# A batched x·yᵀ kernel on one core: TensorE's unrolled stream becomes a loop of three iterations over four groups of 8 heads, with credit semaphores

## The chip, the cores and the metric

The kernel runs on one core of a Trainium2 chip. The metric is the device time of one execution in microseconds, the median of several. A run is compared with executions of the kernel before in the same rounds on the same chip.

Short names: PE is TensorE's matrix multiply and PEld its weight load, DVE is VectorE, ACT is ScalarE, POOL is GpSimd, and SP is SyncE, which issues the DMAs.

## The reference

```python
x, y: (8, 12, 512, 64) float32          # batch, heads, rows, channels
out = np.einsum('bhtc,bhsc->bhts', x, y)  # (8, 12, 512, 512) float32
```

There are 96 independent products of 512x64 by 64x512. The inputs are 25 MB and the output is 101 MB, so the output dominates the traffic.

## The kernel before

Twelve groups of eight heads are handled one after the other. For each group the kernel loads x and y as 128 partitions of 4 KB rows (`a` selects one of two tiles of four heads), casts them to bf16 on GpSimd, transposes them on TensorE and copies them out of PSUM as `xT` and `yT`. Then it runs 16 matmul steps. A step is 8 matmuls into a PSUM tile of 128x1024, which ACT and DVE copy in turn into an output tile of 4 MB. The output tile is stored by one DMA; the first and the last tile are stored in four pieces of 1 MB. Tile, the framework, orders all of this and sets the semaphores.

```python
for g in range(NG):                                   # 12 groups
    steps = prepare(g + 1, made) ...                  # loads, casts, transposes of the next group
    for a in range(2):
        ot = opool.tile([P, R, S], fp32)              # 4 MB, three buffers
        for k in range(K):                            # 8 steps
            if k in (0, 3, 6): next(steps, None)
            pm = pmpool.tile([P, 2, S], fp32)         # three buffers
            for two in range(2):
                for h in range(G):                    # 4 heads: 32 columns of weights each
                    nc.tensor.matmul(pm[h*Q:(h+1)*Q, two, :],
                                     xT[a*C:(a+1)*C, 2*k+two, h*Q:(h+1)*Q],
                                     yT[a*C:(a+1)*C, h*S:(h+1)*S], start=True, stop=True)
            # ACT (even k) or DVE (odd k) copies pm into ot
        nc.sync.dma_start(ov[g, a], otf)              # (...) four pieces at both ends
```

## Time and profile before

| | before |
|---|---|
| time, median | 307.29 us of 3 runs (307.26 to 307.49) |
| span of the profiled execution | 305.6 us |
| instructions | 4,378, of which 3,840 are TensorE's matmuls and weight loads |
| DMA | 126.11 MB, 413 GB/s on average |

These lines of the page of the kernel before give, in order, the span, busy time of each engine, the DMA engines' busy tenths and their GB/s in 40 equal slices, and two DMA queues (packets, MB, share of 16 engines' span).

```profile
span 305.6 us, 4378 instructions
PE 203.8 (67%) x1920; PEld 91.5 (30%) x1920; DVE 138.4 (45%) x120; ACT 119.6 (39%) x121; POOL 49.3 (16%) x54
...
DMA  7999999999999999999999999999999999999980
GB/s 278 412 409 420 459 419 399 470 418 388 446 455 388 440 446 398 441 429 437 427 424 442 420 427 430 411 454 420 437 435 425 427 442 422 437 437 422 409 368 39
...
q1 hardware_dynamic: 10848, 125.83, 97.2%
q8 instruction: 15, 0.25, 0.3%
```

No compute engine is busy for more than two thirds of the span. DMA is at 90% or more in all but the first slice and the last two. (Bytes are counted in the slice in which their packet starts, so a single slice can read high: 16 engines that move 32 KB in 1213 ns each make 432 GB/s.) Queue q8 carries instruction fetches, 15 blocks of 16 KB. The waits view of the same kernel agrees (engine, line, what it waited for; us in total, times, longest).

```profile
ACT ot L129 <- DMA out_dram<-ot: 72.1, 11, 9.9
...
PE pm L122 <- ACT ot L129: 64.7, 14, 9.7
DVE ot L131 <- DMA out_dram<-ot: 63.4, 15, 9.3
```

ACT and DVE wait for a store to land before they may refill an output buffer, and PE waits behind ACT.

The following windows of the kernel before give the stretch, its length, busy time of each engine, the granted clock, the DMA share and GB/s.

```profile
290.00:295.00 5.00, 0.00 (x0) 0.00 (x0) 0.00 (x0) 0.00 (x0) 0.00 (x0) 0.50 1.00 423
...
297.00:298.00 1.00, 0.00 (x0) 0.00 (x0) 0.00 (x0) 0.00 (x0) 0.00 (x0) 0.50 0.50 213
...
300.00:301.00 1.00, 0.00 (x0) 0.00 (x0) 0.00 (x0) 0.00 (x0) 0.00 (x0) 0.50 0.06 25
...
303.00:304.00 1.00, 0.00 (x0) 0.00 (x0) 0.00 (x0) 0.00 (x0) 0.00 (x0) 0.50 0.06 25
304.00:305.00 1.00, 0.00 (x0) 0.00 (x0) 0.00 (x0) 0.00 (x0) 0.00 (x0) 0.50 0.00 0
```

A share of 0.06 is one DMA engine of 16. From 300 to 304 us the whole kernel waits for a single DMA engine. By the packet records it had no more to move than the others: its packets of 32 KB are 176 of 2,816, a sixteenth. So this one was slower. We call it the **late engine**.

**How the late engine was followed.** The trace has a record of every DMA packet (start, duration, size, queue), without the engine's number. On a busy engine a packet starts 3 to 4 ns before the one ahead of it ends, and the sizes of the packets are on record (a store of 4 MB is 128 packets of 32 KB, of which the chain has eight). So the chain can be followed back from the very last packet. In the kernel before it is a chain without a gap (but for one 0.3 us interruption by a packet of queue q14) from 1.88 us to 304.22 us. A 32 KB packet takes 1213 ns on nearly all engines. On the late engine it takes that too at times, but mostly 50 to 90 ns more. These durations are our own sums over the packet records, as no view prints them.

### The profile page before, as it was taken

The page shows a single profiled execution, that of the slowest core. Times are in us where ns is not written, and L with a number is a line of the kernel's source. Part 1 is how long each engine was busy: PE and PEld are TensorE (multiplying, and loading weights), DVE is VectorE, ACT ScalarE, POOL GpSimd, SP SyncE. Part 2 cuts the span into 40 slices and gives each one's busy share as a digit, 9 for nine tenths or more (in the row PEclk, how much of TensorE's full clock was granted, in tenths as well). Part 3 has the DMA queues.
Part 4 walks back from the last instruction along what each step waited for, and adds up shares of the span by engine and source line. Part 5 has one row for each costly group of instructions (what it writes and reads, how often), then busy time and mean ns, then how long its engine had stood idle before and what let it go on. Part 6 is the DMA issues. An engine that isn't in the chain of part 4 may idle for free.

```text
span 305.6 us, 4378 instructions
## 1 busy us (share of the span) xinstructions
PE 203.8 (67%) x1920; PEld 91.5 (30%) x1920; DVE 138.4 (45%) x120; ACT 119.6 (39%) x121; POOL 49.3 (16%) x54
## 2 busy tenths in 40 slices
PE   1899999969919928936932990991785976575000
PEld 1443234525404503512511540350251432222000
DVE  0465654657416507615633741670664664446000
ACT  1445527544523606505522451560653463325000
POOL 3755024300500500320140050041000000000000
PEclk9999999975555555755675555575575555555555
DMA  7999999999999999999999999999999999999980
GB/s 278 412 409 420 459 419 399 470 418 388 446 455 388 440 446 398 441 429 437 427 424 442 420 427 430 411 454 420 437 435 425 427 442 422 437 437 422 409 368 39
DMA packets 10867, 126.11 MB, mean 413 GB/s; under 512 B 864, under 2 KB 864, under 8 KB 7008
## 3 DMA queue, kind: packets, MB, share of 16 engines
q1 hardware_dynamic: 10848, 125.83, 97.2%
q8 instruction: 15, 0.25, 0.3%
q14 instruction: 4, 0.03, 0.0%
HBM read 25.17 MB, written 100.66 MB: 412 GB/s over the span
## 4 chain that ended last, share of the span: by engine, by line
DMA 49%; PE 29%; DVE 5%; issue 4%; ACT 3%; POOL 1%; SPq 0%; ACTq 0%
DMA out_dram<-ot 47%; PE pm L122 23%; DVE ot L131 5%; PE pt L95 4%; ACT ot L129 3%; PE pt L82 2%; DMA xs<-in_x_dram 2%; ACT xT L102 1%; POOL xb L73 1%; DVE xT L100 0%; SPq L55 0%; ACTq L129 0%; SPq L136 0%
## 5 line engine op out<-in xcount | busy, mean ns | idle before, releaser
L122 PE MATMUL pm<-yT,xT 64*32 64x512 bf16 x1536 | 159.4, 586 | 67.2 <-ACT ot L129 64.7
L131 DVE COPY ot<-pm 128x1024 f32<-128x1024 f32 x96 | 117.0, 1224 | 123.0 <-DMA out_dram<-ot 63.4
L129 ACT ACTIVATE ot<-pm 128x1024 f32<-128x1024 f32 x96 | 95.9, 1023 | 115.5 <-DMA out_dram<-ot 72.1
L122 PEld LDWEIGHTS <-xT 64*32 64x32 bf16 x1536 | 53.3, 118 | 148.1 <-issue 136.3
L73 POOL CAST yb<-ys 128x1024 bf16<-128x1024 f32 x24 | 24.3, 1040 | 143.5 <-PE pt L82 69.8
L82 PE MATMUL pt<-ident,yb 128*128 128x128 bf16 x192 | 23.9, 297 | 8.5 <-POOL yb L73 6.8
L102 ACT ACTIVATE xT<-pt 128x1024 bf16<-128x1024 bf16 x12 | 12.3, 1023 | 37.0 <-PE pt L95 30.3
L95 PE MATMUL pt<-ident,xb 128*128 128x128 bf16 x192 | 25.8, 310 | 1.3 <-DVE xT L100 0.8
L73 POOL CAST xb<-xs 128x1024 bf16<-128x1024 f32 x24 | 24.3, 1040 | 13.7 <-issue 4.9
L95 PEld LDWEIGHTS <-xb 128*128 128x128 bf16 x192 | 19.4, 143 | 22.7 <-issue 20.0
L82 PEld LDWEIGHTS <-yb 128*128 128x128 bf16 x192 | 19.3, 138 | 17.7 <-issue 8.2
L88 DVE COPY yT<-pt 128x1024 bf16<-128x1024 bf16 x12 | 14.6, 1216 | 8.5 <-PE pt L82 8.5
L90 ACT ACTIVATE yT<-pt 128x1024 bf16<-128x1024 bf16 x12 | 12.2, 1019 | 8.2 <-PE pt L82 8.2
L100 DVE COPY xT<-pt 128x1024 bf16<-128x1024 bf16 x12 | 8.3, 690 | 12.3 <-PE pt L95 9.8
L90 ACT ACT_TABLE_LOAD x1 | 1.3, 1283 | 0.7 <-PEq L151 0.7
masks.py:199 POOL TENSOR_SCALAR_AFFINE_SELECT ident<-ident 128x128 bf16<-128x128 bf16 x1 | 0.3, 292 | 0.1
masks.py:197 POOL MEMSET ident<- 128x128 bf16 x1 | 0.2, 204 | 0.3 <-POOLq L151 0.3
L151 POOL MEMSET const-float32-0.0<- 128x1 f32 x1 | 0.1, 98 | 0.2 <-issue 0.2
L151 POOL MEMSET const-bfloat16-1.0<- 128x1 bf16 x1 | 0.1, 101 | 0.0
L151 POOL MEMSET const-uint8-127<- 128x1 uint8 x1 | 0.1, 101 | 0.0
L151 POOL MEMSET const-float32-1.0<- 128x1 f32 x1 | 0.1, 98 | 0.0
## 6 DMA issues: line engine op xcount, KB each, us to landing
out_dram<-ot SPq DMA_DIRECT2D x22, 4096.0 KB, 27.4
ys<-in_y_dram SPq DMA_DIRECT2D x12, 1024.0 KB, 21.2
xs<-in_x_dram SPq DMA_DIRECT2D x12, 1024.0 KB, 23.4
out_dram<-ot SPq DMA_DIRECT2D x8, 1024.0 KB, 19.2
```

The costliest lines, as they stand in the source:

```text
L73: nc.gpsimd.tensor_copy(b[:, rows], s[:, :, rows].rearrange("p a r c -> p r a c"))
L82: nc.tensor.transpose(pt[:, k, :], yb[:, half * K + k].rearrange("p a c -> p (a c)"), ident)
L88: nc.vector.tensor_copy(dst, src)
L90: nc.scalar.activation(dst, src, COPY)
L95: nc.tensor.transpose(pt[:, k, :], xb[:, half * K + k].rearrange("p a c -> p (a c)"), ident)
L100: nc.vector.tensor_copy(dst, pt)
L102: nc.scalar.activation(dst, pt, COPY)
L122: nc.tensor.matmul(pm[h * Q:(h + 1) * Q, two, :], xT[a * C:(a + 1) * C, 2 * k + two, h * Q:(h + 1) * Q], yT[a * C:(a + 1) * C, h * S:(h + ...
L129: nc.scalar.activation(ot[:, 2 * k:2 * k + 2, :], pm, COPY)
L131: nc.vector.tensor_copy(ot[:, 2 * k:2 * k + 2, :], pm)
L151: nc = _bacc.Bacc("TRN2", target_bir_lowering=False, num_devices=1)
```

## The change

The intent is to save instruction fetches: TensorE gets a loop of three iterations whose body is four groups, and the other engines stay unrolled. The waits in this loop body are written with fixed counts, the same in all three iterations, so TensorE takes *credits*: it waits for a semaphore to be at least 1 (or 4) and subtracts that again. Tile cannot express this, so everything sits in one critical section with hand-made semaphores.

```diff
-    for g in range(NG):
-        (...)                       # Tile's pools, tiles and waits
+    with tc.tile_critical():
+        (...)                       # 32 semaphores, SP and POOL unrolled
+        def take(name, n=1):
+            pe.wait_ge(S_(name), n)
+            pe.sem_inc(S_(name), -n)
+        (...)
+        with pe.Fori(0, NG // BODY):              # 3 iterations
+            for i in range(BODY):                 # 4 groups
+                t = i % NT
+                take("T", 4)                      # all four copies of this group
+                for n in range(2 * K):
+                    a, k = divmod(n, K)
+                    if n in AT:                   # n = 2, 5, 8, 11
+                        transposes(i + 1, AT[n])  # takes c.. and pt..; a 13th, empty group at the end
+                    m = (i * 2 * K + n) % 3
+                    take(f"pm{m}")
+                    (...)                         # the same 8 matmuls
+                    ins.then_inc(S_("ma" if k % 2 == 0 else "mv"), 1)
+        (...)                       # ACT and DVE unrolled:
+            copy(eng, dst, src).then_inc(S_(f"pt{j % 2}"), 1)
+            eng.drain().then_inc(S_("T"), 1)
```

Data, layouts, buffers and DMA sizes stay. The load of a later group is issued somewhat later than before (SP's timeline has the fourth load of y at 12.01 us, not 7.75): behind the store of the group's first tile, and after the transposes that free its buffer.

More of the change, by code (lines that the diff above doesn't have):

```diff
@@ L6 @@
 from concourse._compat import with_exitstack
-from concourse.masks import make_identity
 @with_exitstack
@@ L31 @@
     K = R // 2
-    AHEAD = 3
+    BODY = 4
+    NL = 3
+    NO = 3
+    NT = 2
     fp32 = mybir.dt.float32
@@ L35 @@
     COPY = mybir.ActivationFunctionType.Copy
-    assert C * 2 == P and S == T and R == 16
+    assert C * 2 == P and S == T and R == 16 and NG % BODY == 0
     xv = x.rearrange("b h t c -> (b h t c)").rearrange("(g a p n) -> g p a n", a=2, p=P, n=R * C)
     yv = y.rearrange("b h t c -> (b h t c)").rearrange("(g a p n) -> g p a n", a=2, p=P, n=R * C)
-    ov = out.rearrange("b h t s -> (b h t s)").rearrange("(g a p n) -> g a p n", a=2, p=P, n=R * S)
-    const = ctx.enter_context(tc.tile_pool(name="const", bufs=1))
@@ L43 @@
-    lpool = ctx.enter_context(tc.tile_pool(name="lpool", bufs=AHEAD))
-    bpool = ctx.enter_context(tc.tile_pool(name="bpool", bufs=2))
-    tpool = ctx.enter_context(tc.tile_pool(name="tpool", bufs=2))
-    opool = ctx.enter_context(tc.tile_pool(name="opool", bufs=3))
-    ptpool = ctx.enter_context(tc.tile_pool(name="ptpsum", bufs=2, space=bass.MemoryType.PSUM))
-    pmpool = ctx.enter_context(tc.tile_pool(name="pmpsum", bufs=3, space=bass.MemoryType.PSUM))
-    loaded = {}
-    def load(g):
-        xs = lpool.tile([P, 2, R, C], fp32)
-        ys = lpool.tile([P, 2, R, C], fp32)
-        nc.sync.dma_start(ys.rearrange("p a r c -> p a (r c)"), yv[g])
-        nc.sync.dma_start(xs.rearrange("p a r c -> p a (r c)"), xv[g])
-        loaded[g] = (xs, ys)
@@ L59 @@
-    for g in range(AHEAD):
-        load(g)
-    ident = const.tile([P, P], bf16)
-    make_identity(nc, ident)
-    def prepare(g, made):
-        xs, ys = loaded.pop(g)
-        yb = bpool.tile([P, R, 2, C], bf16)
-        xb = bpool.tile([P, R, 2, C], bf16)
-        for s, b in ((ys, yb), (xs, xb)):
-            for half in range(2):
-                rows = slice(half * K, (half + 1) * K)
-                nc.gpsimd.tensor_copy(b[:, rows], s[:, :, rows].rearrange("p a r c -> p r a c"))
-        if g + AHEAD < NG:
-            load(g + AHEAD)
-        yield
-        yT = tpool.tile([P, G * Q, R], bf16)
-        xT = tpool.tile([P, R, P], bf16)
-        for half in range(2):
-            pt = ptpool.tile([P, K, P], bf16)
+    ov = out.rearrange("b h t s -> (b h t s)").rearrange("(o p n) -> o p n", p=P, n=R * S)
@@ new lines @@
+    sb = ctx.enter_context(tc.tile_pool(name="sb", bufs=1))
+    ps = ctx.enter_context(tc.tile_pool(name="ps", bufs=1, space=bass.MemoryType.PSUM))
+    ident = sb.tile([P, P], bf16)
+    xs = sb.tile([P, NL, 2, R, C], fp32)
+    ys = sb.tile([P, NL, 2, R, C], fp32)
+    xb = sb.tile([P, NT, R, 2, C], bf16)
+    yb = sb.tile([P, NT, R, 2, C], bf16)
+    xT = sb.tile([P, NT, R, P], bf16)
+    yT = sb.tile([P, NT, G * Q, R], bf16)
+    ot = sb.tile([P, NO, R, S], fp32)
+    pt = ps.tile([P, 2, K, P], bf16)
@@ new lines, with S_, store_cuts, load @@
+    pm = ps.tile([P, 3, 2, S], fp32)
+    sem = {}
+    def S_(name):
+        if name not in sem:
+            sem[name] = tc.alloc_semaphore(name)
+        return sem[name]
+    def store_cuts(o):
+        n = 4 if o in (0, 2 * NG - 1) else 1
+        return [(i * R // n, (i + 1) * R // n) for i in range(n)]
+    landed = [16 * sum(len(store_cuts(i)) for i in range(o % NO, o + 1, NO)) for o in range(2 * NG)]
+    with tc.tile_critical():
+        for name in ("ident", "T", "ma", "mv", "oa", "ov"):
+            S_(name)
+        for j in range(4):
+            S_(f"t{j}")
+            for t in range(NT):
+                S_(f"c{j}{t}")
+        for i in range(NL):
+            S_(f"ldx{i}"), S_(f"ldy{i}")
+        for i in range(NO):
+            S_(f"st{i}")
+        for i in range(2):
+            S_(f"pt{i}")
+        for i in range(3):
+            S_(f"pm{i}")
+        def load(g):
+            i = g % NL
+            if g >= NL:
+                nc.sync.wait_ge(S_("t1"), g - NL + 1)
+                nc.sync.wait_ge(S_("t3"), g - NL + 1)
+            nc.sync.dma_start(ys[:, i].rearrange("p a r c -> p a (r c)"), yv[g]).then_inc(S_(f"ldy{i}"), 16)
+            nc.sync.dma_start(xs[:, i].rearrange("p a r c -> p a (r c)"), xv[g]).then_inc(S_(f"ldx{i}"), 16)
+        for g in range(NL + 1):
+            load(g)
+        done = 0
+        for o in range(2 * NG):
+            if o % 2 == 1 and o // 2 + NL + 1 < NG:
+                load(o // 2 + NL + 1)
+            of = ot[:, o % NO].rearrange("p r s -> p (r s)")
+            for a, b in store_cuts(o):
+                done += 1
+                nc.sync.wait_ge(S_("oa"), done)
+                nc.sync.wait_ge(S_("ov"), done)
+                nc.sync.dma_start(ov[o][:, a * S:b * S], of[:, a * S:b * S]).then_inc(S_(f"st{o % NO}"), 16)
+        for o in range(2 * NG - NO, 2 * NG):
+            nc.sync.wait_ge(S_(f"st{o % NO}"), landed[o])
+        nc.gpsimd.memset(ident, 0.0).then_inc(S_("ident"), 1)
+        nc.gpsimd.wait_ge(S_("ident"), 1)
+        nc.gpsimd.affine_select(
+            out=ident, in_=ident, compare_op=mybir.AluOpType.not_equal, fill=1.0, base=0,
+            pattern=[[-1, P]], channel_multiplier=1,
+        ).then_inc(S_("ident"), 1)
+        for g in range(NG + 1):
+            i, t = g % NL, g % NT
+            for j in range(4):
+                s, b, ld = ((ys, yb, "ldy"), (xs, xb, "ldx"))[j // 2]
+                if j % 2 == 0 and g < NG:
+                    nc.gpsimd.wait_ge(S_(f"{ld}{i}"), 16 * (g // NL + 1))
+                if g >= NT:
+                    nc.gpsimd.wait_ge(S_(f"t{j}"), g - NT + 1)
+                if g < NG:
+                    rows = slice(j % 2 * K, (j % 2 + 1) * K)
+                    nc.gpsimd.tensor_copy(
+                        b[:, t, rows], s[:, i, :, rows].rearrange("p a r c -> p r a c")
+                    ).then_inc(S_(f"c{j}{t}"), 1)
+                else:
+                    nc.gpsimd.sem_inc(S_(f"c{j}{t}"), 1)
+        pe = nc.tensor
+        def take(name, n=1):
+            pe.wait_ge(S_(name), n)
+            pe.sem_inc(S_(name), -n)
+        def transposes(i, j):
+            t, b = i % NT, (yb, xb)[j // 2]
+            take(f"c{j}{t}")
+            take(f"pt{j % 2}")
@@ L81, in prepare @@
             for k in range(K):
-                nc.tensor.transpose(
-                    pt[:, k, :], yb[:, half * K + k].rearrange("p a c -> p (a c)"), ident
-                )
-            dst = yT[:, :, half * K:(half + 1) * K]
-            src = pt.rearrange("p k n -> p n k")
-            if half == 0:
-                nc.vector.tensor_copy(dst, src)
-            else:
-                nc.scalar.activation(dst, src, COPY)
-            yield
-        for half in range(2):
-            pt = ptpool.tile([P, K, P], bf16)
-            for k in range(K):
-                nc.tensor.transpose(
-                    pt[:, k, :], xb[:, half * K + k].rearrange("p a c -> p (a c)"), ident
-                )
-            dst = xT[:, half * K:(half + 1) * K]
-            if half == 0:
-                nc.vector.tensor_copy(dst, pt)
-            else:
-                nc.scalar.activation(dst, pt, COPY)
-            yield
@@ L104, in prepare @@
-        made[g] = (xT, yT.rearrange("p n k -> p (n k)"))
-    made = {}
-    for _ in prepare(0, made):
-        pass
-    for g in range(NG):
-        xT, yT = made.pop(g)
-        steps = prepare(g + 1, made) if g + 1 < NG else iter(())
-        for a in range(2):
-            ot = opool.tile([P, R, S], fp32)
-            otf = ot.rearrange("p r s -> p (r s)")
-            edge = (g == 0 and a == 0) or (g == NG - 1 and a == 1)
-            for k in range(K):
-                if k in (0, 3, 6):
-                    next(steps, None)
-                pm = pmpool.tile([P, 2, S], fp32)
-                for two in range(2):
-                    for h in range(G):
-                        nc.tensor.matmul(
-                            pm[h * Q:(h + 1) * Q, two, :],
-                            xT[a * C:(a + 1) * C, 2 * k + two, h * Q:(h + 1) * Q],
-                            yT[a * C:(a + 1) * C, h * S:(h + 1) * S],
-                            start=True, stop=True,
-                        )
-                if k % 2 == 0:
-                    nc.scalar.activation(ot[:, 2 * k:2 * k + 2, :], pm, COPY)
-                else:
-                    nc.vector.tensor_copy(ot[:, 2 * k:2 * k + 2, :], pm)
-                if edge and k % 2 == 1:
-                    i, j = (2 * k - 2) * S, (2 * k + 2) * S
-                    nc.sync.dma_start(ov[g, a][:, i:j], otf[:, i:j])
-            if not edge:
-                nc.sync.dma_start(ov[g, a], otf)
@@ new lines, in transposes @@
+                ins = pe.transpose(
+                    pt[:, j % 2, k], b[:, t, j % 2 * K + k].rearrange("p a c -> p (a c)"), ident
+                )
+            ins.then_inc(S_(f"t{j}"), 1)
+        pe.wait_ge(S_("ident"), 2)
+        for i in range(2):
+            pe.sem_inc(S_(f"pt{i}"), 1)
+        for i in range(3):
+            pe.sem_inc(S_(f"pm{i}"), 1)
+        for j in range(4):
+            transposes(0, j)
+        AT = {2: 0, 5: 1, 8: 2, 11: 3}
+        with pe.Fori(0, NG // BODY):
[8 more added lines that the diff above has]
+                    take(f"pm{m}")
+                    for two in range(2):
+                        for h in range(G):
+                            ins = pe.matmul(
+                                pm[h * Q:(h + 1) * Q, m, two, :],
+                                xT[a * C:(a + 1) * C, t, 2 * k + two, h * Q:(h + 1) * Q],
+                                yT[a * C:(a + 1) * C, t, h * Q:(h + 1) * Q].rearrange("c n k -> c (n k)"),
+                                start=True, stop=True,
+                            )
+                    ins.then_inc(S_("ma" if k % 2 == 0 else "mv"), 1)
@@ new lines, in copy, with evacuate @@
+        def copy(eng, dst, src):
+            if eng is nc.scalar:
+                return eng.activation(dst, src, COPY)
+            return eng.tensor_copy(dst, src)
+        def evacuate(eng, g, j):
+            t = g % NT
+            eng.wait_ge(S_(f"t{j}"), g + 1)
+            if g == NG:
+                if j < 2:
+                    eng.sem_inc(S_(f"pt{j}"), 1)
+                return
+            if j < 2:
+                dst, src = yT[:, t, :, j * K:(j + 1) * K], pt[:, j].rearrange("p k n -> p n k")
+            else:
+                dst, src = xT[:, t, (j - 2) * K:(j - 1) * K], pt[:, j - 2]
+            copy(eng, dst, src).then_inc(S_(f"pt{j % 2}"), 1)
+            eng.drain().then_inc(S_("T"), 1)
@@ new lines @@
+        for eng, first, ready, stored in (
+            (nc.vector, 1, "mv", "ov"),
+            (nc.scalar, 0, "ma", "oa"),
+        ):
+            mine = (0, 2) if eng is nc.vector else (1, 3)
+            for j in mine:
+                evacuate(eng, 0, j)
+            waiting = []
+            for o in range(2 * NG):
+                g, a = divmod(o, 2)
+                if o >= NO:
+                    eng.wait_ge(S_(f"st{o % NO}"), landed[o - NO])
+                cuts = [b for _, b in store_cuts(o)]
+                for k in range(first, K, 2):
+                    n = a * K + k
+                    m = (g % BODY * 2 * K + n) % 3
+                    for at, j in AT.items():
+                        if j in mine and at in (n, n - 1):
+                            evacuate(eng, g + 1, j)
+                    eng.wait_ge(S_(ready), o * (K // 2) + k // 2 + 1)
+                    copy(eng, ot[:, o % NO, 2 * k:2 * k + 2], pm[:, m]).then_inc(S_(f"pm{m}"), 1)
+                    if 2 * k + 2 in cuts or 2 * k + 4 in cuts:
+                        eng.drain().then_inc(S_(stored), 1)
```

## The prediction

> **What bounds the kernel now.** DMA. The page's slices show the 16 DMA engines 90% busy or more from 8 to 290 us; the mean is 413 GB/s over 126.11 MB, and the data queue takes 97.2% of 16 engines' span. [...] one-microsecond windows of this trace reach 418 to 426. PE is 67% busy, DVE 45%, ACT 39%. By the waits view ACT waits 72.1 us and DVE 63.4 us for a store to land before they refill an output buffer, and PE 64.7 us for ACT; the chain is 47% output stores.
>
> The end is set by one engine. In one-microsecond windows the DMA share falls from 0.89 at 295 us to 0.06 (one engine of 16) from 300 to 304 us. In the packet records most engines finish at 295.5 to 299 us, one at 304.2. A 32 KB store packet takes 1213 ns nearly everywhere; one engine's take about 1274 ns, some 110 times, about 8 us in all with its smaller packets.
>
> **What the change does.** The DMA view shows 15 instruction fetches of 16 KB, which is TensorE's 3,840 matmuls and weight loads (0.3% of DMA time). A fetch takes about 1 us and delays one DMA engine by 1.4 to 1.6 us; different engines are hit, and I find no hit on the late one. The loop body of four groups is about 1,280 matmuls and weight loads and some 200 semaphore instructions. [...] no run here shows yet whether iterations two and three are fetched again. If they are: as many fetches as before, and a stall of a few us (estimate, from 1 us a fetch) at two back edges near 110 and 210 us, where two stores of 9.7 us each are queued. If not, some 9 fetches go. Either way not on the engine that ends last.
>
> Added: per step a wait and a decrement on PE (estimate 0.05 to 0.2 us, 1 to 3 us a group), drains on ACT and DVE, one wait for all four transpose copies before a group's first matmul (about 1 us later in group 0: one more ACT copy of 1.02 us). PE has 100 us of slack, so none of it counts while DMA has a backlog. That is thin only at the head: five groups' loads and the first store (14.7 MB at 424 GB/s from 2.3 us) last to 37 us; the second store was issued at 32.9 us. PE is busy without a break there, so a first group slower by over 4 us would open a DMA gap. I expect about 1 us, no gap.
>
> **Prediction.** Nothing of weight leaves the critical path. 307.5 us, range 306.2 to 309.5. Faster by over 2%: 0.02; within 2%: 0.93; slower by over 2%: 0.05.
>
> **What would show it.** The data queue again near 97%; ACT and DVE still waiting longest for stores; the last microseconds again with one engine of 16 busy; the second store issued before 37 us; fetches at 15 to 19 (refetched) or about 6 (kept), without change of time.
>
> **What would make it wrong.** PE's semaphore pairs costing over 0.3 us a step; a DMA gap at 33 to 47 us; fetches falling on the slow engine (1.4 us each); its longer packets going away (up to 8 us faster); a late first load.

307.5 us is 0.2 us over the 307.29 us of the kernel before. The estimate of 0.05 to 0.2 us a step is the author's; in the trace of the kernel before, the three semaphore instructions on TensorE took 51 ns each. The 15 fetches took 0.88 to 1.08 us each in that trace.

## The result, and the profile after

The changed kernel took 309.84 us (median of 4, 309.57 to 309.98), and the kernel before in the same rounds 307.39 us (307.26 to 307.75). The ratio is 1.0077, with a 95% interval of 1.0059 to 1.0094. Such a ratio is the mean time of one kernel's fast runs over that of the other's of the same rounds, so it is not quite the ratio of the medians. Executions over 1.5% slower than the fastest of the same kernel are left out of the means. The change costs 2.45 us, clear of the scatter, and ends 0.3 us outside the predicted range. It is still "within 2%".

The page of the changed kernel:

```profile
span 308.0 us, 4846 instructions
PE 224.6 (73%) x1952; PEld 88.4 (29%) x1952; DVE 139.6 (45%) x120; ACT 120.7 (39%) x121; POOL 49.6 (16%) x54
...
DMA  7999999999999999999999999999999999999950
GB/s 266 412 408 428 451 413 458 380 452 449 384 446 434 406 450 426 417 448 421 447 405 430 447 412 427 447 396 447 448 426 426 438 434 438 426 427 444 397 235 19
...
q1 hardware_dynamic: 10848, 125.83, 96.5%
q8 instruction: 5, 0.08, 0.1%
```

The intent worked: 5 fetches in place of 15. All five lie before 93 us in the packet records, so iterations two and three fetched nothing. There are 468 more instructions. The second store was issued at the same moment in both kernels, as SP's timeline shows (start, duration, engine, line, operation), before and then after:

```profile
32.88 0.33 SPq L136 DMA_DIRECT2D out_dram<-ot  x1
```

```profile
32.88 10.76 SPq L110 DMA_DIRECT2D out_dram<-ot  x2
```

The first store was issued 0.7 us later (16.60 us, not 15.90), about as predicted, and by the second store nothing of that was left. The window from 33 to 47 us shows no DMA gap (share, then GB/s, at the end of the line; changed kernel; before, the share was 1.03). The windows after it are of its tail:

```profile
33.00:47.00 14.00, 13.44 (x118) 5.77 (x119) 7.94 (x7) 6.78 (x8) 3.56 (x4) 1.00 1.05 444
...
298.00:299.00 1.00, 0.00 (x0) 0.00 (x0) 0.00 (x0) 0.00 (x0) 0.00 (x0) 1.00 0.16 66
299.00:300.00 1.00, 0.00 (x0) 0.00 (x0) 0.00 (x0) 0.00 (x0) 0.00 (x0) 1.00 0.06 25
...
305.00:306.00 1.00, 0.00 (x0) 0.00 (x0) 0.00 (x0) 0.00 (x0) 0.00 (x0) 1.00 0.06 25
306.00:307.00 1.00, 0.00 (x0) 0.00 (x0) 0.00 (x0) 0.00 (x0) 0.00 (x0) 1.00 0.00 0
```

The tail is the interesting part. Fifteen engines finish *earlier* than before (the share is down to one engine at 299 us, not 300), and the sixteenth works alone for seven microseconds in place of four.

The chain view is of no use after the change: it names 5% of the span and stops, as it cannot follow the hand-made semaphores.

```profile
PE 5%; DVE 0%; issue 0%
PE pm L175 4%; PE pt L150 1%; DVE ot L187 0%
```

From the packet records, the span splits into three parts:

| us | before | changed | difference |
|---|---|---|---|
| up to the late engine's first packet | 1.88 | 2.05 | +0.17 |
| the late engine's chain of packets, without gaps | 302.34 | 303.93 | +1.59 |
| after its last packet | 1.39 | 1.97 | +0.59 |
| span | 305.61 | 307.95 | +2.35 |

The first and the last part are the critical section's entry and exit. SP's first DMA was issued at 0.95 us, not 0.74, behind a handshake of the engines; and after the last landing there is another handshake, with the clearing of more semaphores on POOL (244 ns, not 98). The middle part is the question. The chain has the same packets in both kernels; 1.45 us of its 1.59 us are longer packets after the first load, and 0.21 us are longer packets in the first load (successive packets overlap by 0.06 us more in all).

**Theory A, from the trace of before.** Look at the late engine's 176 store packets of 32 KB and count the instructions of all engines that end while each is under way. Packets with no instruction beside them (38) are 2.4 ns over 1213 on average; packets with 26 to 33 instructions beside them (44) are 68 ns over. A straight line through all of them has a slope of 2.4 ns an instruction (correlation 0.91); in the changed kernel it is 2.3 ns (0.86). So each executed instruction, of whatever engine, would cost the late engine about 2 ns, and with it the kernel, since the late engine is never idle. 468 more instructions would cost about 1 us.

**Rivals.** B: TensorE's pace, slowed by credits, reaches the end through the buffers. C: only fixed costs of start, end and loop. D and E: the loop's back edges, or the fetches. F: TensorE's work (its reads, its power) lengthens the packets, not the count of instructions.

### The profile page after: what moved, and what is told of

Read it like the earlier page. It is cut to its first block, busy times and chain, and to the rows that moved or that the text cites. A ratio compares the mean times of both kernels' runs of the same rounds, so it can differ in the third digit from the quotient of the medians.

```text
span 308.0 us, 4846 instructions
## 1 busy us (share of the span) xinstructions
PE 224.6 (73%) x1952; PEld 88.4 (29%) x1952; DVE 139.6 (45%) x120; ACT 120.7 (39%) x121; POOL 49.6 (16%) x54
## 3 DMA queue, kind: packets, MB, share of 16 engines
q1 hardware_dynamic: 10848, 125.83, 96.5%
## 5 line engine op out<-in xcount | busy, mean ns | idle before, releaser
L175 PE MATMUL pm<-yT,xT 64*32 64x512 bf16 x1536 | 176.8, 624 | 49.1 <-PEq L142 45.1
L187 DVE COPY ot<-pm 128x1024 f32<-128x1024 f32 x96 | 117.5, 1224 | 117.3 <-PE pm L175 58.9
L186 ACT ACTIVATE ot<-pm 128x1024 f32<-128x1024 f32 x96 | 96.6, 1023 | 152.3 <-DMA out_dram<-ot 89.5
L175 PEld LDWEIGHTS pm<-yT,xT 64*32 64x32 bf16 x1536 | 48.2, 124 | 144.9 <-issue 143.2
L150 PE MATMUL pt<-ident,yb 128*128 128x128 bf16 x208 | 26.8, 310 | 7.3 <-PEq L142 7.3
L150 PE MATMUL pt<-ident,xb 128*128 128x128 bf16 x208 | 27.0, 310 | 1.5 <-issue 0.9
L150 PEld LDWEIGHTS pt<-ident,yb 128*128 128x128 bf16 x208 | 20.1, 141 | 27.2 <-issue 27.2
L150 PEld LDWEIGHTS pt<-ident,xb 128*128 128x128 bf16 x208 | 20.1, 142 | 21.1 <-issue 21.1
```

Of the source, the lines that this page charges most:

```text
L150: ins = pe.transpose(pt[:, j % 2, k], b[:, t, j % 2 * K + k].rearrange("p a c -> p (a c)"), ident)
L175: ins = pe.matmul(pm[h * Q:(h + 1) * Q, m, two, :], xT[a * C:(a + 1) * C, t, 2 * k + two, h * Q:(h + 1) * Q], yT[a * C:(a + 1) * C, t, h * ...
L186: return eng.activation(dst, src, COPY)
L187: return eng.tensor_copy(dst, src)
```

## The experiments

### 1 and 2. Empty instructions (void as a dose, useful as repeats)

```diff
+                    for _ in range(4):
+                        pe.nop(nofuse=True)
                     take(f"pm{m}")
```

The second has 16 of them on GpSimd before each cast.

> The changed kernel with four empty instructions before each of the 192 matmul steps on TensorE (768 more instructions). Theory A (an instruction tax on the late DMA engine: each instruction that the core executes lengthens one DMA engine's packets by 2.3 to 3 ns, and that engine's unbroken chain of packets is the whole span): 1.8 to 2.3 us slower than the changed kernel, 311.6 to 312.1 us, and the late engine's excess over 1213 ns a packet grows by as much. Rival B (TensorE's pace reaches the end through the buffers): slower too, by TensorE's extra time at the head only. Rival C (only fixed costs of start, end and loop): 309.8 us.

> The changed kernel with 16 empty instructions on GpSimd before each cast (832 more instructions, on an engine that is idle 84% of the time; TensorE's stream is untouched). Theory A: 1.9 to 2.5 us slower, 311.7 to 312.3 us, as with TensorE's. Rival B (TensorE's pace): no change, 309.8 us. Rival C: 309.8 us.

Measured: 309.79 us and 309.97 us. The pages list 4,846 and 4,874 instructions: the compiler had dropped the empty ones (the 28 more of the second are semaphore instructions on GpSimd). The runs say nothing of the theory. They are two repeats of the changed kernel (309.84 us), and show how far its time and its trace scatter: the late engine's excess was 10.15 us in the first trace, 10.01 and 9.75 us in these.

### 3. TensorE's loop unrolled

```diff
-        with pe.Fori(0, NG // BODY):
+        for _ in range(NG // BODY):
```

> The changed kernel with TensorE's loop unrolled by Python: same instructions and semaphores, no loop. Instruction fetches go from 5 back to some 16. Theory A: within 0.5 us of 309.8 us, as the instruction count stays (1.4 us more for each fetch that happens to hit the late DMA engine). Rival D (the loop itself, its back edges, costs the 2.4 us): back to 307.4 us. Rival E (fetches cost the end): slower by several us.

Measured: 310.31 us (309.92 to 310.68) with 4,839 instructions and 16 fetches. Rival D falls: taking out the loop does not bring the time back. Rival E falls too: 11 more fetches did not cost several microseconds. The 0.47 us that it is slower has a likely cause: in its trace three load packets of the late engine were stretched by 1.4 us together (at 62 and 88 us), which none of the other traces has to that extent. We did not trace them to a fetch.

### 4. A quarter of the matmuls, with a wrong result on purpose

```diff
-                        for h in range(G):
+                        for h in range(1):
                             ins = pe.matmul(
-                                pm[h * Q:(h + 1) * Q, m, two, :],
-                                xT[a * C:(a + 1) * C, t, 2 * k + two, h * Q:(h + 1) * Q],
+                                pm[:, m, two, :],
+                                xT[a * C:(a + 1) * C, t, 2 * k + two, :],
```

> The changed kernel with one matmul of 128 columns in place of four of 32, which gives a wrong result on purpose (the right shape, all of PSUM written); 2304 instructions fewer, DMA unchanged. Theory A: 5.3 to 6.9 us faster than the changed kernel, 303 to 304.5 us, where the other DMA engines (done at 299 us in the changed kernel's trace) are next. Rival B: at most the 307.4 us of before. Rival C: 309.8 us.

Measured: 305.48 us (305.28 to 305.75), 4.4 us faster than the changed kernel, and 1.9 us faster than the kernel before. Its page:

```profile
span 303.7 us, 2542 instructions
PE 220.3 (73%) x800; PEld 83.2 (27%) x800; DVE 139.7 (46%) x120; ACT 120.7 (40%) x121; POOL 49.4 (16%) x54
```

This is less than the 5.3 to 6.9 us expected, or 1.9 ns for each of the 2,304 instructions. PE's modelled busy time hardly changed (220.3 against 224.6 us), so this run alone already speaks against rivals B and F. Rival C alone is excluded: its fixed costs are all still there.

### 5 and 6. Real semaphore increments, on TensorE and on GpSimd

Two dummy semaphores are incremented, and nobody waits on them: four increments before each matmul step on TensorE (768 more), or 16 before each cast on GpSimd.

```diff
+                    for z in range(4):
+                        pe.sem_inc(S_(f"d{z % 2}"), 1)
                     take(f"pm{m}")
```

> The changed kernel with four real semaphore increments (two dummy semaphores that nobody waits on) before each of the 192 matmul steps on TensorE: 768 more instructions, none of which moves data. The empty instructions of the first try were dropped by the compiler, so this is that test again. Theory A (instruction tax on the late DMA engine, 2.05 ns an instruction by the run with one matmul, 2.3 by the packets of one trace): 1.6 to 1.8 us slower than the changed kernel, 311.4 to 311.8 us. Rival F (TensorE's work, not its instructions, lengthens the packets): 309.8 us.

> The changed kernel with 16 real semaphore increments before each cast on GpSimd: 812 more instructions there, TensorE untouched. Theory A: 1.7 to 1.9 us slower, 311.5 to 311.9 us. Rivals B (TensorE's pace) and F (TensorE's work): 309.8 us.

Measured: 311.58 us (311.46 to 311.77) and 311.57 us (311.33 to 311.63), both about 1.7 us over the changed kernel and inside what theory A said. Here are the span and queue lines of the run on TensorE, then of the run on GpSimd, which leaves TensorE's stream alone:

```profile
span 309.8 us, 5614 instructions
...
q1 hardware_dynamic: 10848, 125.83, 95.8%
```

```profile
span 309.5 us, 5658 instructions
...
q1 hardware_dynamic: 10848, 125.83, 96.0%
```

POOL is busy for 16% of the span and waits most of the rest; instructions that move no data, on an engine off the critical path, make the kernel slower. Rivals B and F cannot explain that. In the run on GpSimd the tail is the late engine's again:

```profile
301.00:302.00 1.00, 0.00 (x0) 0.00 (x0) 0.00 (x0) 0.00 (x0) 0.00 (x0) 1.00 0.06 25
...
306.00:307.00 1.00, 0.00 (x0) 0.00 (x0) 0.00 (x0) 0.00 (x0) 0.00 (x0) 1.00 0.08 33
307.00:308.00 1.00, 0.00 (x0) 0.00 (x0) 0.00 (x0) 0.00 (x0) 0.00 (x0) 1.00 0.02 8
```

### 7. Fewer matmuls with a right result, first try (loads of 64 partitions)

If instructions are the cost, halving the matmuls should beat the kernel before. Two heads are put on the two halves of the 128 rows, with block-diagonal weights, so that two summed matmuls do the work of four. In this try the stacking was done by the loads:

```diff
-    xv = (...).rearrange("(g a p n) -> g p a n", a=2, p=P, n=R * C)
+    xv = (...).rearrange("(g u a p n) -> g u p a n", u=2, a=2, p=P // 2, n=R * C)
-        nc.sync.dma_start(xs.rearrange(...), xv[g])
+            for u in range(2):
+                nc.sync.dma_start(s[u * C:(u + 1) * C].rearrange(...), v[g, u])
```

> The kernel before with two heads' channels in one matmul (block-diagonal weights of 128 rows and 128 columns, two matmuls summed in PSUM, where there were four of 64 rows and 32 columns): half the matmuls, 1536 instructions fewer, [...] the loads are 48 of half the size, and each xT copy is two of 64 partitions. Right result. Theory A: the late engine's excess falls by about 3 us, 304.0 to 304.8 us, if no other engine ends later. Rivals B and F [...]: 307.4 us or a little more.

Measured: 350.47 us (343.65 to 353.26), right, and far slower. Three of its four executions, the profiled one among them, were slow, so no ratio is given. The cause shows inside the one trace: while only loads run, DMA moves half as much as in the kernel before. First this run, then the kernel before:

```profile
3.00:14.00 11.00, 2.07 (x17) 1.60 (x18) 6.83 (x3) 1.02 (x1) 3.17 (x4) 1.00 1.03 226
```

```profile
12.00:14.00 2.00, 2.00 (x22) 0.75 (x24) 0.00 (x0) 1.77 (x2) 1.46 (x2) 1.00 1.03 412
```

The 16 engines are as busy as ever, at 226 in place of 412 GB/s, as 4 KB packets take 302 ns in the median and not 159. Why loads of 64 partitions have longer packets was not shown. The run says nothing of theory A.

### 8. Sparing the late engine in the last stores

```diff
                 if edge and k % 2 == 1:
+                    if g > 0 and k > 1:
+                        nc.sync.dma_start(ov[g, a][:120, i:j], otf[:120, i:j])
+                        nc.sync.dma_start(ov[g, a][120:, i:j], otf[120:, i:j])
+                    else: (...)
```

> The kernel before with three of the last four stores of 1 MB each split into partitions 0 to 119 [...] and 120 to 127 [...]. [...] the end moves to the next late engine, near 301 us in the trace, and the time to 304.0 to 305.0 us. [...]

The split was meant to leave the late engine out of the larger store. 304.0 to 305.0 us is the estimate for the case that this succeeds.

Measured: 314.20 us (312.8 to 314.28), 6.8 us slower than the kernel before (ratio 1.0208, 1.0184 to 1.0232). One engine works alone at the end, for longer than before:

```profile
304.00:308.00 4.00, 0.00 (x0) 0.00 (x0) 0.00 (x0) 0.00 (x0) 0.00 (x0) 0.50 0.06 25
308.00:312.00 4.00, 0.00 (x0) 0.00 (x0) 0.00 (x0) 0.00 (x0) 0.00 (x0) 0.50 0.05 20
```

In the packet records that last engine moved nine packets a piece, eight and then one, so it took part in both stores of each piece. Followed back as above, its excess is 8.6 us with 4,381 instructions, which makes it the late engine: it was not spared. Some 6 us more came from packets that were stretched just where stores of the old and the new split overlapped (two of 32 KB by 2.45 and 1.45 us). Why they were stretched was not shown. As a way to balance the engines, this failed.

### 9. The unrolled form without credits

```diff
         def take(name, n=1):
-            pe.wait_ge(S_(name), n)
-            pe.sem_inc(S_(name), -n)
+            taken[name] = taken.get(name, 0) + n
+            pe.wait_ge(S_(name), taken[name])
```

> The unrolled form of the changed kernel (310.3 us) with the credits taken out: TensorE waits for absolute counts, and nearly all these waits ride on the matmuls; 244 instructions fewer, all of them TensorE's semaphore decrements. Theory A at 2.2 ns an instruction (from the two runs with added increments): 0.5 us faster than the unrolled one, near 309.8 us. Rival C (fixed costs of the critical section, 0.8 us at start and end, and the rest from the credits' waiting): 308.2 us.

Measured: 308.68 us (308.62 to 308.92, 5 runs), 1.6 us faster than the unrolled form with credits (310.31 us) and 1.2 us faster than the changed kernel. It lies between what theory A and rival C said. By A the 244 instructions are worth 0.5 us, and the stretched packets of the unrolled run's trace 1.4 us; or else a credit costs more than another instruction. Against the kernel before it has 217 instructions more, worth 0.45 us at 2.05 ns (the mean found below); with the 0.76 us of the critical section's entry and exit that makes 1.2 us, and 1.28 us were measured. Experiment 12 tests the price of a credit by itself.

### 10. Fewer matmuls with a right result, second try

The loads are as before. The copies out of PSUM stack the heads: four copies of 64 partitions in place of one of 128.

```diff
+    wide = [const.tile([P, R, 2, 2, P], bf16, name=f"wide{i}") for i in range(2)]   # zeroed once
+            for a in range(2):
+                for s in range(2):
+                    copy(half, xT[s*C:(s+1)*C, half*K:(half+1)*K, a, :, s*2*Q:s*2*Q+Q],
+                         pt[a*C:(a+1)*C, :, s*2*Q:(s+1)*2*Q].rearrange("p k (h q) -> p k h q", q=Q))
     (...)                           # yT likewise
-                    for h in range(G):
+                    for h in range(2):
                         nc.tensor.matmul(
-                            pm[h * Q:(h + 1) * Q, two, :], (...)
-                            start=True, stop=True,
+                            pm[:, two, :],
+                            xT[:, 2 * k + two, a, h * (P - Q):h * (P - Q) + P],
+                            yT[:, a, h],
+                            start=h == 0, stop=h == 1,
```

> The kernel before with its 128-partition loads kept, and two heads of one output tile stacked by the copies out of PSUM (four copies of 64 partitions and half the elements in place of one), so that two summed matmuls of 128 rows and 128 columns do the work of four: 768 matmuls and 768 weight loads fewer, 144 copies more, about 1370 instructions fewer; DMA unchanged. Right result. Theory A at 2.2 ns an instruction: 3.0 us faster than before, 304.4 us, unless another DMA engine (the latest of the others ended 4 us before the last) comes last. Rival F [...]: 307.4 us.

Measured: right, 304.98 us (304.93 to 305.22), ratio to the kernel before 0.9921 (0.9908 to 0.9935), 2.4 us faster where 3.0 were expected. Its page:

```profile
span 303.2 us, 2979 instructions
PE 212.8 (70%) x1130; PEld 103.2 (34%) x1152; DVE 176.2 (58%) x194; ACT 153.0 (50%) x193; POOL 49.4 (16%) x54
```

PE, PEld, DVE and ACT are all busier than in the kernel before, and the kernel is faster. (Rival F's 307.4 us took TensorE's time as unchanged, a premise that was not shown; PE was busy for 212.8 us here and for 203.8 us in the kernel before.) (Some 22 matmul records are missing from this trace.) It beats both kernels.

### 11. The same, with loads of 8 KB rows

```diff
-    xv = (...).rearrange("(g a p n) -> g p a n", a=2, p=P, n=R * C)
+    xv = (...).rearrange("(g p n) -> g p n", p=P, n=2 * R * C)
     (...)                           # the copies interleave even and odd row blocks; 96 more of them
```

> As the run before, and the loads take 8 KB rows (32 rows of one head to a partition) in place of 4 KB ones: a 4 KB packet took 159 ns and an 8 KB one 309 ns, so each DMA engine's 24 loads take 24 x (16 x 159 - 8 x 309) ns = 1.7 us less; 96 copies more. Theory A: 304.4 - 1.7 + 0.2 = 302.9 us. Rival F: 305.7 us. Where the copies slow the first group by over 4 us, a gap at the head would eat it.

Measured: right, 305.59 us (304.39 to 305.83), ratio 0.9932. The load packets did not keep their 309 ns: from 25 to 150 us they averaged 322 to 325 ns (their 95th percentile is 407 to 416 ns), and the gain of 1.7 us did not come. It is 0.6 us slower than experiment 10. Why the packets are stretched is left open.

### 12. Added credits

```diff
+                    for z in range(4):
+                        take(f"d{z % 2}")         # the dummies start at 1000, no wait ever blocks
                     take(f"pm{m}")
```

> The changed kernel with four more credits before each of the 192 matmul steps on TensorE: 768 instructions that each wait for a dummy semaphore to be 1 or more and take 1 off it; the dummies start at 1000, so none ever waits. It is the test with added increments again, with the very instruction that the change added. Taking the credits out of the unrolled form gave 1.6 us for 244 instructions, 6.7 ns each, where an increment cost 2.2 ns. Theory A1 (a credit costs the late DMA engine what any instruction costs, 1.95 to 2.3 ns; the rest of those 1.6 us was three stretched load packets in the unrolled run's trace, 1.4 us): 1.5 to 1.8 us slower than the changed kernel, 311.3 to 311.6 us. Theory A2 (a credit costs three times as much): 4.5 to 5 us slower, 314.3 to 314.9 us.

Measured: 311.65 us (311.51 to 312.03), 1.8 us over the changed kernel for 768 credits, 2.4 ns each. A credit costs the end what a plain increment costs. The median is 0.05 us above the range of theory A1 and far from that of A2; a dear credit is excluded, and of the 1.6 us of experiment 9 about 1.1 us must have been something else that the unrolled run had, most likely those stretched packets.

### All traces together

The late engine was followed in ten traces, of eight different programs; the experiments ran on four chips, and every trace that was followed has such an engine. The excess is all time of its packets over 159, 309 and 1213 ns (4, 8 and 32 KB), without the first load and without single packets that were over by more than 0.2 us.

```
kernel                     instructions   excess us   median time us
one matmul of four (4)             2542        5.41           305.48
stacked by copies (10)             2979        6.25           304.98
before                             4378        8.69           307.39
no credits, unrolled (9)           4595        8.97           308.68
unrolled (3)                       4839        9.45           310.31
changed                            4846       10.15           309.84
changed, repeat (1)                4846       10.01           309.79
changed, repeat (2)                4874        9.75           309.97
increments on TensorE (5)          5614       12.00           311.58
increments on GpSimd (6)           5658       11.82           311.57
```

The least-squares line is excess = 2.05 ns x instructions - 0.03 us (correlation 0.988, scatter 0.3 us). Extended to no instructions, it passes within 0.03 us of zero. So not only the difference between the kernels but the late engine's whole lag of about 9 us scales with the number of instructions that the core executes.

The traces allow one more test, packet by packet (our own sums again). In the trace of the kernel before, 175 of the late engine's 176 packets of 32 KB, all stores (the one beside the packet of q14 is left out), are sorted by the number of instructions that ended while the packet ran. The fifth with fewest (none) is over 1213 ns by 2 ns on average, the fifth with most (27 to 46) by 71 ns; over all 175 the correlation is 0.89, and in the traces of experiments 1, 2, 4, 5, 9, 10 and 12 it is 0.77 to 0.92. After the last copy out of PSUM, at 282.2 us, the engine's 42 remaining packets are over by 48 ns in all. Packets of 32 KB on other engines are over by 0.1 ns on average. So the time is added when instructions run, and on this engine. It is added to stores: the engine's 4 KB load packets are over by 2.1 ns (1.7 ns on the others), although 3.2 instructions ended during each. The 2.05 ns are thus a mean over all instructions; those that ended during the 32 KB stores cost 2.5 ns each.

The trace of experiment 12, which is not in the fit, agrees: about 12.1 us of excess with 5,616 instructions, where the line gives 11.5 us.

What stands behind it is not shown. Lengths over 1213 ns come in steps of about 9.4 ns (1265, 1274, 1284, 1293), and the 4-byte packets of the same trace take 9 ns; that these two figures are close is all that the records show. Every execution quoted here, timed or profiled, comes with a span and a granted clock, so none went unrecorded, and none shows whether an unrecorded one would pay the tax. That stays open, and with it whether the 2.4 us gained by experiment 10 would be seen there.

## Why the prediction was right or wrong

It said 307.5 us, at most 309.5, and 309.84 came.

- **Right: what bounds the kernel, and that one engine sets its end.** The last microseconds again show a share of 0.06. The data queue is at 96.5%. By the waits view ACT again waits longest for stores (89.5 us), and DVE's waits for stores (72.2 us on two tiles) exceed its longest other wait (58.9 us for PE).
- **Right: the fetches.** 5 in place of 15 ("about 6 (kept)"), and no change of time from it, as none is on the late engine's chain. The loop body of about 1,400 instructions was fetched once, where the unrolled form had 16 fetches. The unrolled forms fit that: with 16 fetches 0.47 us slower than the changed kernel, with stretched load packets in the trace; with 15 fetches and 251 instructions fewer, 1.2 us faster.
- **Right: no DMA gap at the head.** The second store was issued at 32.88 us in both kernels. The credits' own time on TensorE (51 ns each in the trace, one instruction for wait and decrement, 0.05 to 0.2 us expected) is off the critical path.

This line of the source view of the changed kernel gives the credit instructions' count and duration (ns; min, median, max):

```profile
L142 PEldq EVENT_SEMAPHORE  x308: 51/51/51, 7.1 to 281.2; - x154
```

- **Wrong: "so none of it counts while DMA has a backlog".** This step failed. The added instructions were costed as time on their own engines, which have slack, and in that place they cost nothing. They cost on the late DMA engine, whose store packets get longer as instructions run, on TensorE and on GpSimd alike (1.7 us for 768 and for 812 added ones). The prediction had seen that engine's long packets and taken their 8 us as a given. They are about 2 ns for each of 4,378 instructions. The change adds 313 semaphore instructions on TensorE, 110 drains on DVE and ACT and 64 instructions for the transposes of a thirteenth group that does not exist, and saves some elsewhere: 468 in all, worth 0.96 us by the line above.
- **Mis-sized: fixed costs.** The prediction named "a late first load" only as a risk and gave the critical section's exit nothing. The trace shows 0.17 us at the start and 0.59 us at the end.
- **The sum.** 0.17 + 0.59 + 0.96 = 1.72 us of the 2.35 us in the span. Another 0.21 us are longer packets in the first load, whose cause was not tested. The rest, some 0.4 us, is of the size of the scatter around the line (before lies 0.28 us below it, the changed kernel 0.22 us above). We leave it open.
- The granted clock rose from 0.634 to 1.000 with the change. It does not explain the cost of instructions: the runs with added instructions were at 1.000 as well and differ from the changed kernel by 1.7 to 1.8 us. Whether it has a part in the 0.4 us left open is not shown.

## What to carry to other kernels

Where DMA is the limit, look at the last microseconds in fine windows: if a single DMA engine ends last, its chain is the critical path, and savings elsewhere, here ten instruction fetches, are worth nothing. On such a kernel count instructions, those of idle engines too (tested here on TensorE and GpSimd): in executions recorded as these are, 2 ns each on the critical chain, so that a version with 1,400 fewer instructions won 0.8% although its compute engines were busier. When restacking data, compare the rate of the loads first: here loads of 64 partitions ran at 226 GB/s, those of 128 at 412.
